# Two-layer diffusion-transformer block on eight cores: stages over all tokens, side work woven between main steps, two even FFN blocks, address tracking in place of barriers

## The chip, the cores and the metric

The kernel runs on the eight cores of one Trainium2 chip, which form two dies (cores 0 to 3 and 4 to 7). Each core computes half of the latent tokens of one of four samples, and no core waits for another. Each has a matmul engine (PE, with its weight loads shown apart as PEld), a vector engine (DVE), a scalar engine (ACT), a GpSimd engine (POOL, used here to issue the weight DMAs) and a sync engine (SP, used for the other DMAs).

The metric is the device time of the slowest core in microseconds (us). Executions come in a fast and a slow state; in the slow one the cores of one die, or of both, show a lower granted clock and the time is some per cent longer.

## The reference, cut to what matters

```python
D_MODEL, SEQ, CTX_LEN, HEAD_DIM = 2048, 4096, 256, 128
ATT_Q_HEADS, ATT_KV_HEADS, FFN_HIDDEN, WINDOW = 12, 4, 5632, 128

for i in range(2):                                   # two layers (shortened)
    mod  = silu(c) @ w_mod + b_mod                   # 6 x 2048: shift, scale, gate, twice
    cmod = silu(c_ctx) @ w_mod + b_mod               # the same for the context tokens
    xn = rms_norm(h) * (1 + scale1) + shift1
    # layer 0: q, k (per-head RMS norm, rotary), v; full attention over 256 context + 4096 latent keys;
    #          a gated width-3 convolution of 512 channels beside it
    # layer 1: the same heads, keys within 128 positions + the context keys, a learned sink per head;
    #          a multi-scale mean pooling of 512 channels beside it
    h = h + gate1 * (concat(attention, aux) @ w_out)
    hn = rms_norm(h) * (1 + scale2) + shift2
    h = h + gate2 * ((silu(hn @ w_gate) * (hn @ w_up)) @ w_down)
    # layer 0 does all this for the context tokens too; layer 1 only reads their keys and values
return rms_norm(h)                                   # latent tokens
```

A core owns 2048 latent tokens, computes 128 more and the 256 context tokens through layer 0 for the sake of layer 1's window and prefix, and needs layer-0 keys and values of all 4352 tokens.

## The kernel before: the parts that matter

A small scheduler appends instructions to one list per engine and derives semaphore waits from named buffer slots. Where buffers are reused under other names, a barrier makes every engine wait for all earlier work. **In the timelines read below, each engine executes its list in the order in which the program appended to it** (a DVE step that needs nothing of the three steps of 0.6 us before it starts only after them, and ACT stands still for 5.29 us meanwhile); everything below turns on that.

The program goes through layer 0 in three token blocks (1024, 1024 and 128 + 256), with attention, output projection and FFN in each:

```python
for b in range(3):
    c0 = 0
    for si_, sb in enumerate(subs0[2 * b:2 * b + 2]):
        stage1(0, sb, c0, mod_part=2 * b + si_)     # attention, w_out, mods, second norm
        c0 += sb["n"]
    sc.barrier()
    hcol = subs0[2 * b]["hcol"]
    segs = [(0, c0, 0)] if b < 2 else [(0, 128, 0), (128, 384, 1)]
    stage2(0, hcol, c0, segs)                       # FFN of this block
    sc.barrier()
```

The norm's second half, which writes the normalised activations, is a pair of steps per 128 channels: a multiplication on DVE, then an addition of the shift on ACT.

```python
for c in range(KD):                                 # norm_finish, 16 chunks of 128 channels
    ti = 1 + (c % 2)
    sc.op("dve", lambda e, c=c, ti=ti: e.scalar_tensor_tensor(
        out=tmp[ti][:, 0:n], in0=Xb[:, c, 0:n], scalar=dcol(acol + c), in1=tmp[0][:, 0:n],
        op0=ALU.mult, op1=ALU.mult), ...)
    sc.op("act", lambda e, c=c, ti=ti: e.activation(
        out=dst[:, c, dst_c0:dst_c0 + n], in_=tmp[ti][:, 0:n], func=AF.Identity,
        bias=dcol(bcol + c), scale=1.0), ...)
```

The key and query heads go through a three-deep pipeline, `proj_heads`. `A` is the per-head norm (square on ACT, a matmul with ones on PE, logarithm and exponential on ACT, a multiplication on DVE, a copy on ACT), `B` the rotary part (a matmul on PE, then three DVE steps).

```python
proj(0)
if ni > 1:
    proj(1)
for i in range(ni):
    A(i)
    if i + 2 < ni:
        proj(i + 2)
    B(i)
```

## Time and profile before

Four executions took 10001.53 to 10074.45 us, with a median of 10005.08 us.

| before, core 4 (the slowest of the profiled run) | |
|---|---|
| PE busy | 7548.1 us of 10077.9 (75%) |
| PE waits for w_mod tiles | 501.4 us |
| PE waits in the FFN's down product for the reloaded residual | 303.6 us |
| a dense FFN stretch, 2660 to 2968 us | 1406 matmuls in 308 us, clock 0.99 |
| the third FFN block (384 tokens), 5660 to 6400 us | PE busy 435.9 of 740 us, clock 0.78 |
| the three layer-0 FFN blocks | 1057 + 1055 + 713 = 2825 us |

The last row is read in the chain of waits, from the first wait for a gate tile to the last store of a block. The page's first lines give the busy time of the engines, then the PE row and the clock row in 40 slices of the span (digits are tenths):

```profile
span 10077.9 us, 109258 instructions; the slowest of 8 cores (9996.4 to 10077.9 us)
...
PE 7548.1 (75%) x37188; PEld 3431.9 (34%) x37188; DVE 2363.6 (23%) x4252; ACT 2513.5 (25%) x3658; POOL 529.4 (5%) x454
...
PE   2665486879897868899955456557699994679897
...
PEclk9777798989998979899976678778899997889998
```

The FFN blocks are the stretches of eights and nines in the PE row; the low slices between them are norms, mod products and attention preludes, and the run of fives in the middle holds the third FFN block. Groups of the same page, with busy time, mean ns of one, and idle time of the engine before the group with its main cause:

```profile
L450 PE MATMUL pair<-arena 128*128 128x512 bf16 (+2 forms) x624 | 282.0, 486 | 536.0 <-ACT arena L445 323.8
...
L409 PE MATMUL pair<-arena 128*128 128x2 bf16 x3072 | 87.8, 165 | 501.4 <-DMA arena<-w_mod 501.4
```

The matmuls with ones of the norms (L450) find PE idle for 536 us, nearly twice their busy time; the mod products (L409) keep PE busy 88 us and idle 501 us. Two windows, with columns as named in their first line:

```profile
core 4: us, PE busy (x) PEld busy (x) DVE busy (x) ACT busy (x) POOL busy (x), PEclk, DMA share, GB/s
2660.00:2968.00 308.00, 305.59 (x1406) 137.96 (x1407) 32.05 (x46) 23.88 (x44) 22.08 (x19) 0.99 0.57 78
5660.00:6400.00 740.00, 435.90 (x2320) 233.01 (x2320) 57.03 (x118) 27.95 (x54) 75.09 (x63) 0.78 0.94 132
```

In the dense stretch a 512-column matmul starts every 308 / 1406 = 0.219 us. In the 384-token block the DMA engines are busy 94% of the time: all FFN weights are read for few tokens.

### The profile page before, as it was taken

The page shows a single profiled execution, that of the slowest core. Times are in us where ns is not written, and L with a number is a line of the kernel's source. Part 1 is how long each engine was busy: PE and PEld are TensorE (multiplying, and loading weights), DVE is VectorE, ACT ScalarE, POOL GpSimd, SP SyncE. Part 2 cuts the span into 40 slices and gives each one's busy share as a digit, 9 for nine tenths or more (in the row PEclk, how much of TensorE's full clock was granted, in tenths as well). Part 3 has the DMA queues.
Part 4 walks back from the last instruction along what each step waited for, and adds up shares of the span by engine and source line. Part 5 has one row for each costly group of instructions (what it writes and reads, how often), then busy time and mean ns, then how long its engine had stood idle before and what let it go on. Part 6 is the DMA issues. An engine that isn't in the chain of part 4 may idle for free.

```text
span 10077.9 us, 109258 instructions; the slowest of 8 cores (9996.4 to 10077.9 us)
## 1 busy us (share of the span) xinstructions
PE 7548.1 (75%) x37188; PEld 3431.9 (34%) x37188; DVE 2363.6 (23%) x4252; ACT 2513.5 (25%) x3658; POOL 529.4 (5%) x454
## 2 busy tenths in 40 slices
PE   2665486879897868899955456557699994679897
PEld 1222232334342323344433333223244441234342
DVE  2222143421112434111122100234411113430102
ACT  2223274810002837100023100234510003430000
POOL 0000000000000000000000011000000000000000
PEclk9777798989998979899976678778899997889998
DMA  8777847375757373857677899654466666555756
GB/s 153 136 137 126 138 107 148 105 117 78 127 84 152 102 142 101 123 94 112 93 152 154 127 127 124 132 114 96 97 95 109 97 114 154 110 93 70 135 70 166
DMA packets 1251085, 1186.96 MB, mean 118 GB/s; under 512 B 54128, under 2 KB 1098352, under 8 KB 1250544
## 3 DMA queue, kind: packets, MB, share of 16 engines
q0 software_dynamic: 988320, 659.35, 48.7%
q1 hardware_dynamic: 262224, 520.62, 16.5%
q8 instruction: 312, 5.11, 0.2%
q14 instruction: 229, 1.88, 0.1%
HBM read 1684.66 MB, written 154.53 MB: 182 GB/s over the span
## 4 chain that ended last, share of the span: by engine, by line
PE 53%; DMA 33%; DVE 6%; ACT 4%; issue 3%; another core or an unknown queue 1%; SPq 0%; DVEq 0%; ACTq 0%; POOL 0%; POOLq 0%
PE pair L924 25%; DMA arena<-hT_d 8%; DMA hT_d<-arena 7%; PE pair L485 7%; PE pair L881 5%; PE pair L687 4%; PE pair L717 4%; DMA arena<-w_mod 4%; DMA arena<-w_gate 4%; DMA arena<-kT_d 2%; DVE arena L964 2%; PE pair L726 2%; DMA arena<-v_d 2%; PE pair L621 2%; ACT arena L467 2%
## 5 line engine op out<-in xcount | busy, mean ns | idle before, releaser
L924 PE MATMUL pair<-arena 128*128 128x512 bf16 (+1 forms) x12672 | 2723.8, 379 | 200.9 <-DMA arena<-w_up 139.4
L924 PEld LDWEIGHTS pair<-arena 128*128 128x128 bf16 x12672 | 1254.2, 99 | 1668.9 <-issue 279.1
L955 PE MATMUL pair<-arena 128*128 128x512 bf16 (+1 forms) x6336 | 1450.8, 394 | 321.8 <-DVE arena L964 303.6
L701 ACT ACTIVATE arena<-pair 128x1024 bf16<-128x1024 f32 (+2 forms) x1224 | 1077.5, 907 | 354.1 <-PE pair L687 250.6
L933 ACT ACTIVATE arena<-pair 128x512 f32<-128x512 f32 (+1 forms) x396 | 212.6, 583 | 3467.6 <-PE pair L924 3467.6
L485 PE MATMUL pair<-arena 128*128 128x512 bf16 (+2 forms) x4032 | 859.8, 374 | 286.2 <-ACT arena L467 246.3
L955 PEld LDWEIGHTS pair<-arena 128*128 128x128 bf16 x6336 | 641.2, 102 | 1131.4 <-issue 494.9
L687 PE MATMUL pair<-arena 128*128 128x512 bf16 (+1 forms) x2436 | 691.1, 385 | 273.9 <-DMA arena<-v_d 271.1
L936 DVE TENSOR_TENSOR arena<-pair,arena 128x512 bf16<-128x512 f32 (+1 forms) x396 | 268.0, 677 | 2551.9 <-PE pair L924 2533.3
L717 PE MATMUL pair<-arena 128*128 128x512 bf16 (+3 forms) x2436 | 678.6, 357 | 127.7 <-ACT arena L701 82.8
L445 ACT ACTIVATE arena<-arena 128x512 bf16<-128x512 f32 (+2 forms) x312 | 181.7, 582 | 2182.4 <-DMA arena<-hT_d 670.1
L450 PE MATMUL pair<-arena 128*128 128x512 bf16 (+2 forms) x624 | 282.0, 486 | 536.0 <-ACT arena L445 323.8
L485 PEld LDWEIGHTS pair<-arena 128*128 128x128 bf16 x4032 | 399.9, 103 | 705.3 <-issue 352.1
L964 DVE SCALAR_TENSOR_TENSOR arena<-pair,arena 128x512 f32<-128x512 f32 (+1 forms) x320 | 218.8, 684 | 1677.2 <-DMA arena<-hT_d 1513.0
L712 DVE TENSOR_TENSOR arena<-arena 128x512 bf16<-128x512 bf16 (+2 forms) x1080 | 416.8, 386 | 743.5 <-PE pair L717 446.2
L881 PE MATMUL pair<-arena 128*128 128x512 bf16 (+2 forms) x2560 | 524.4, 362 | 30.9 <-DMA arena<-w_out 14.3
L409 PE MATMUL pair<-arena 128*128 128x2 bf16 x3072 | 87.8, 165 | 501.4 <-DMA arena<-w_mod 501.4
L687 PEld LDWEIGHTS pair<-arena 128*128 128x128 bf16 x2436 | 243.0, 105 | 522.8 <-issue 335.4
L464 DVE SCALAR_TENSOR_TENSOR arena<-arena 128x512 f32<-128x512 f32 (+2 forms) x560 | 381.1, 686 | 144.9 <-ACT arena L457 78.9
L467 ACT ACTIVATE arena<-arena 128x512 bf16<-128x512 f32 (+2 forms) x560 | 375.2, 670 | 104.5 <-DVE arena L464 70.3
L726 PE MATMUL pair<-arena 128*128 128x512 bf16 (+2 forms) x1080 | 389.6, 361 | 11.8 <-DVE arena L712 5.8
L717 PEld LDWEIGHTS pair<-arena 128*128 128x128 bf16 x2436 | 232.3, 103 | 419.0 <-issue 244.0
(72 smaller groups left out, 3504.1 us busy)
## 6 DMA issues: line engine op xcount, KB each, us to landing
arena<-w_in POOLq DMA_DIRECT2D x61, 2048.0 KB, 21.0
arena<-w_gate POOLq DMA_DIRECT2D x110, 1024.0 KB, 10.4
arena<-w_up POOLq DMA_DIRECT2D x110, 1024.0 KB, 10.4
arena<-w_down POOLq DMA_DIRECT2D x80, 1408.0 KB, 14.7
arena<-w_mod POOLq DMA_DIRECT2D x48, 2048.0 KB, 30.9
arena<-w_out POOLq DMA_DIRECT2D x40, 2048.0 KB, 15.0
arena<-hT_d SPq DMA_DIRECT2D x132, 512.0 KB, 4.9
hT_d<-arena SPq DMA_DIRECT2D x132, 512.0 KB, 5.0
```

Of the source, the lines that this page charges most:

```text
L464: sc.op("dve", lambda e, c=c, ti=ti: e.scalar_tensor_tensor(out=tmp[ti][:, 0:n], in0=Xb[:, c, 0:n], scalar=dcol(acol + c), in1=tmp[0][:, 0:n],
L467: sc.op("act", lambda e, c=c, ti=ti: e.activation(out=dst[:, c, dst_c0:dst_c0 + n], in_=tmp[ti][:, 0:n], func=AF.Identity, bias=dcol(bcol ...
L485: ins = e.matmul(bk[:, 0:n], lhsT=wt[:, k, cc * 128:(cc + 1) * 128], rhs=src[:, k, c0:c0 + n], start=(k == 0), stop=(k == KD - 1))
L687: sc.op("pe", lambda e, bi_=bi_, k_ap=k_ap: e.matmul(banks[bi_][:, 0:n], lhsT=k_ap, rhs=qa[:, h, 0:n], start=True, stop=True), reads=[s_kv ...
L701: sc.op("act", lambda e, P3=P3, S3=S3, nb_=nb_: e.activation(out=P3[:, 0:nb_, 0:n], in_=S3[:, 0:nb_, 0:n], func=AF.Exp, scale=float(ATT_SC ...
L712: sc.op("dve", lambda e, P3=P3, pq=pq: e.tensor_tensor(out=Psum[pq][:, 0:n], in0=P3[:, 0, 0:n], in1=P3[:, 1, 0:n], op=ALU.add), reads=[s_P ...
L717: sc.op("pe", lambda e, v_ap=v_ap, ti=ti, c0=c0, c1=c1, first=first, last=last, P3=P3: e.matmul(banks[O_b][:, c0:c1], lhsT=v_ap, rhs=P3[:, ...
L726: sc.op("pe", lambda e, pq=pq, dfirst=dfirst, dlast=dlast: e.matmul(banks[D_b][:, 0:n], lhsT=ones, rhs=Psum[pq][:, 0:n], start=dfirst, sto ...
L881: ins = e.matmul(banks[bi_][:, 0:n], lhsT=wt[:, k, c * 128:(c + 1) * 128], rhs=qa[:, k, 0:n], start=(k == 0), stop=(k == KD - 1))
L924: ins = e.matmul(banks[bks[si]][:, 0:b - a], lhsT=wt[:, k, off + c2 * 128:off + (c2 + 1) * 128], rhs=hn[:, k, a:b], start=(k == 0), stop=( ...
L955: ins = e.matmul(banks[yb[si]][:, 0:b - a], lhsT=wt[:, f, c2 * 128:(c2 + 1) * 128], rhs=aT[:, f, a:b], start=(f == 0), stop=(f == 21))
L964: sc.op("dve", lambda e, si=si, a=a, x0=x0, x1=x1, j=j, yb=yb, hi_=hi_, dch=dch: e.scalar_tensor_tensor(out=hb[hi_][:, x0:x1], in0=banks[y ...
```

## The change

The intent is to keep PE fed. The kernel is rewritten so that

- each stage (keys and values, queries, gates, attention with w_out, FFN, layer-1 projections, window attention) runs over all of the core's tokens before the next one starts;
- norms, the mod products, w_out and the pooling become generators ("side" work), and a `weave` emits a given number of their steps per main step into the same instruction lists;
- layer 0's FFN takes two token blocks, 1280 and 1152, in place of three, so its weights are read twice;
- slots carry their addresses, so an access waits for whatever overlaps it and the barriers vanish;
- weights arrive from the host already cut into tiles, in rows of 4 KB and more; attention sums four exponentials before the denominator matmul in place of two, and has two score buffers in place of three.

The diff has 2340 lines. Its core, with cuts marked by "...":

```diff
-    def barrier(self, engs=("pe", "act", "dve", "sp"), skip_keys=("ring0", "ring1", "ring2", "ring3")):
...
+            for o in [s] + s.over:
+                self._wait(eng, o.w)
+                for tok in o.rs.values():
+                    self._wait(eng, tok)
...
+TB = [(0, 1280), (1280, 1152)]
+SPL0 = [[(0, 428), (428, 854), (854, 1280)], [(0, 384), (384, 768), (768, 1152)]]
...
+class Side:
...
+    def weave(self, main, rate):
+        credit = 0.0
+        for _ in main:
+            credit += rate
+            while credit >= 1.0:
+                credit -= 1.0
+                if not self.step():
+                    credit = 0.0
+                    break
...
+    def pipe(items):
...
+        for i in range(n):
+            if items[i].get("A"):
+                items[i]["A"]()
+            if i + 2 < n:
+                proj(i + 2)
+            if items[i].get("B"):
+                items[i]["B"]()
+            yield
...
+    def body():
...
+        stage_a0(side)
+        stage_b0(side)
+        side.weave(ffn_gen(0, 0), 1.6)
+        side.drain()
+        side.add(norm1_gen(0))
+        side.weave(ffn_gen(0, 1), 0.5)
+        side.drain()
+        side.add(norm1_gen(1))
+        stage_a1(side, 0)
+        side.drain()
+        stage_a1(side, 1)
+        stage_b1(side)
+        side.weave(ffn_gen(1, 0), 2.4)
```

`pipe` is the old `proj_heads` with a `yield` at the end of each round: the woven side step is emitted there, after `B(i)` and before `A(i + 1)`. A woven norm step, `apply`, is the same pair as before, DVE then ACT.

## The prediction

> **What bounds the kernel now.** TensorE (PE), and half of that by waiting. The page gives PE busy 7548 us of 10078. The groups show streams of 128x512 matmuls; windows over a dense stretch (2660 to 2968) give 1406 matmuls in 308 us, 218 ns each, at clock 0.99.[...] My estimate by counting moving columns from the code: 31,400 matmuls' worth of 512 columns, 6.8 ms[...]. The other 3.2 ms are idle time and the low clock around it. The waits show where:
> - PE L409 waits 501 us for w_mod tiles (31 us each to landing).
> - The third FFN block (384 tokens, 5660 to 6400) takes 740 us for about 343 us of matmuls; PE waits for w_gate/w_up.
> - FFN down stages take 195 to 215 us per half where 704 matmuls need 152; PE waits for DVE L964, which waits for hT reloads (304 us).
> - RMS norms before each stage: L450 waits 536 us, the first projection after a norm 246 us.
> - k/v reloads per head: L687 waits 271 us, mostly in the 128-token, context and window blocks.
> - The two final norms, about 80 to 95 us each.
>
> **What the change does.** Work falls little: denominator matmuls per quad instead of per pair (-430 units of 512 columns), fewer aux columns, one norm fewer; my count is 30,600 units, 6.6 ms, plus 48 mod tiles now streamed with N=512 (at most 3.5 us each, estimate). The gain is overlap: norms, w_out, mod and k/v loads run beside matmuls, barriers vanish, layer-0 FFN reads weights twice instead of three times with 31 to 35 us of PE work per tile, weights arrive in contiguous 4 KB rows (I expect 12 to 15 us a tile, what w_out needs today).
>
> **Stage by stage (estimates, us).**
> - Start: 8 mod tiles and a norm, 140 (now 230).
> - Layer-0 k/v with woven norm: ACT, DVE and PE all near 33 per 512 tokens; with ordering loss 50 each, 425. Queries: 60 items at the traced 4.2 plus mods, 300. Aux 215.
> - Attention: now 1.08 per key pair, PE-bound (five matmuls). It becomes 4.5, but the exponential itself takes 1.02 plus 0.05 gap, so ACT binds at 1.07: quads gain nothing directly, they make room for w_out. Each 3.5 us w_out chunk starves ACT (two score buffers instead of three). 305 per block; stage 1310, with about 30 lost to mod tiles in the first block.
> - FFN layer 0: 2189 of matmuls, 42 of w_out, 25 exposed per block for loading hn: 2305 (now about 2840).
> - Layer-1 projections 470; window attention and w_out 465.
> - FFN layer 1: 1965 (now about 2015 with final norms).
> - Last final norm: one buffer, 16 serial load-scale-store rounds of 10 to 11: 180, exposed.
> - Unforeseen stalls 105.
>
> Sum 7880 us, range 7500 to 8300; chance of faster by over 2%: 0.97, within 2%: 0.02, slower: 0.01.
>
> **What would show it.** PE busy share near 85 to 88%; FFN windows above 97% PE at clock 0.98 or more; attention windows with exponentials about 1.07 us apart between w_out chunks; w_mod waits under 100 us; no 384-token DMA-bound stage; a PE-idle tail of 150 to 200 us.
>
> **What would make it wrong.** [...]Or w_out and mod chunks placed in PE's order before their weights land, stalling attention; or woven norms delaying projection chains more than I allow; or the serial tail longer.

The 6.8 ms hold: in its densest part, from 2680 to 2880 us at clock 1.00, the trace of before has 928 matmuls of 512 columns in 200 us, 0.216 us each, so that 31,400 take 6.8 ms. Other times of matmuls are estimates of the same kind, a count by the time of one.

Other readings, with what the traces show: an exponential of 1024 columns took 1.022 us in the mean (from 1000 to 1600 us) and twelve in a row took 12.89 us (from 1399.14), 1.07 each. A tile of w_out took a median of 15.0 us to land, one of w_mod 30.9; in the changed kernel it is 19.9 and 20.4, not 12 to 15. The 33 us of the layer-0 keys and values are an estimate for which the prediction names no reading. As to the clock, all eight cores of the kernel before show 0.99 to 1.00 from 2660 to 2968 us. Each core's times count from its own start, and the record does not show when the cores start, so this does not show that they were dense at the same time.

## The result, and the profile after

Four executions of the changed kernel took 8877.16 to 9009.42 us, with a median of 8882.01 us. (In the longest, die 0 has a mean clock of 0.90 in place of 0.92.) The ratio to the kernel before is 0.8898, with a 95% interval from 0.8823 to 0.8973. (A ratio is the mean time of one kernel's fast runs over that of the other's of the same rounds, so it is not quite the ratio of the medians quoted.) It is faster, as predicted, but by about 1120 us and not by the predicted 2125: the time lies outside the predicted range of 7500 to 8300 us.

The lines of the page that answer to those shown of before:

```profile
span 8881.9 us, 100054 instructions; the slowest of 8 cores (8830.8 to 8881.9 us)
...
PE 7197.8 (81%) x35368; PEld 3419.1 (38%) x35368; DVE 2307.6 (26%) x4515; ACT 2313.1 (26%) x3352; POOL 216.9 (2%) x262
...
PE   3556897978877699998999987576556999989993
...
PEclk9778998999998899999999997797777999999996
...
L546 ACT ACTIVATE arena<-arena 128x512 bf16<-128x512 f32 (+6 forms) x448 | 281.7, 630 | 839.0 <-DVE arena L542 823.7
```

PE is busy 81% of the span, not the predicted 85 to 88%. The 384-token hole is gone and the wait for w_mod fell from 501.4 to 131.3 us. But dips remain in slices 1 to 4 and 25 to 31 (counted from one), with a low clock beside most of them: these are the start and layer 0's key stage, the layer-1 projections and the window attention. The last line, the ACT half of the woven norm, shows ACT idle for 823.7 us in front of it, waiting for its DVE half (L542).

The stages in windows (boundaries are the DMA waits that open a stage in the chain of waits): layer-0 keys and values; attention; layer-0 FFN; the two blocks of layer-1 projections; window attention; layer-1 FFN.

```profile
150.00:805.00 655.00, 382.11 (x1352) 147.54 (x1352) 230.15 (x368) 247.39 (x418) 1.75 (x2) 0.78 0.26 73
...
1337.00:2921.00 1584.00, 1250.70 (x5728) 512.34 (x5728) 690.04 (x1616) 998.39 (x1152) 34.96 (x40) 0.93 0.50 116
2921.00:5272.00 2351.00, 2245.75 (x13040) 1268.03 (x13040) 339.03 (x609) 234.20 (x399) 65.73 (x80) 0.98 0.52 111
5272.00:5792.00 520.00, 312.59 (x1184) 138.09 (x1184) 143.85 (x256) 151.03 (x282) 5.25 (x6) 0.74 0.34 84
5792.00:6027.00 235.00, 173.93 (x908) 87.46 (x908) 76.70 (x145) 82.67 (x161) 5.24 (x6) 0.91 0.55 130
6027.00:6743.00 716.00, 417.31 (x1772) 178.49 (x1772) 269.38 (x578) 241.15 (x378) 10.49 (x12) 0.77 0.40 99
6743.00:8735.00 1992.00, 1908.57 (x8783) 849.43 (x8784) 271.08 (x409) 166.12 (x245) 63.11 (x77) 0.98 0.56 121
```

The FFN stages keep PE busy for 2245.75 of 2351 us and 1908.57 of 1992 us at clock 0.98. The others hold PE for 58 to 79% of their time at clocks of 0.74 to 0.93. Against the prediction, stage by stage:

| stage | predicted, us | measured, us | missed by |
|---|---|---|---|
| start | 140 | 150 | 10 |
| layer-0 keys and values, norm woven | 425 | 655 | 230 |
| queries and mods | 300 | 328 | 28 |
| gates and convolution inputs (aux) | 215 | 204 | -11 |
| attention with w_out woven | 1310 | 1584 | 274 |
| FFN layer 0 | 2305 | 2351 | 46 |
| layer-1 projections | 470 | 755 | 285 |
| window attention with w_out woven | 465 | 716 | 251 |
| FFN layer 1 | 1965 | 1992 | 27 |
| last final norm | 180 | 147 | -33 |
| unforeseen stalls | 105 | counted in the rows above | -105 |
| sum | 7880 | 8882 | 1002 |

Four stages carry the miss, and they are the four in which ACT and DVE are busy too and a side generator with DVE and ACT steps is woven in. No one engine's busy time in the windows above fills more than 79% of such a stage. So the loss is in the waits between engines. The waits of PE, the worst first (total us, times, longest us):

```profile
PE pair L479 <- ACT arena L597: 346.0, 74, 13.5
PE pair L479 <- ACT arena L903: 260.6, 163, 5.8
PE pair L479 <- DVE arena L528: 131.6, 85, 4.0
PE pair L479 <- DMA arena<-w_mod: 131.3, 19, 11.7
```

L597 is the square of the per-head norm, L903 the attention's exponential, L528 a square of a woven norm (49.2 of its 131.6 us fall in attention, 34.7 in layer 0's key stage). The timeline shows how 0.5 us of ACT work can hold PE for four. It is one key head of the first layer-1 block (start us, duration, engine, line, operation, idle time before it and what ended that):

```profile
5327.60 5.89 PE L479 MATMUL pair<-arena 128*128 128x428 bf16 x18 [3.86 <-ACT arena L597]
...
5333.67 0.60 DVE L616 TENSOR_TENSOR arena<-pair,arena 128x428 f32<-128x428 f32 x1 [3.42 <-PE pair L479]
5334.19 0.59 DVE L618 TENSOR_TENSOR arena<-arena 128x428 f32<-128x428 f32 x1
5334.96 0.60 DVE L620 TENSOR_TENSOR arena<-arena 128x428 bf16<-128x428 f32 x1 [0.17 <-DVE arena L618]
5335.48 0.61 DVE L542 SCALAR_TENSOR_TENSOR arena<-arena 128x384 f32<-128x384 f32 x1
...
5336.19 0.61 ACT L546 ACTIVATE arena<-arena 128x384 bf16<-128x384 f32 x1 [5.29 <-DVE arena L542]
5336.71 0.51 ACT L597 ACTIVATE arena<-pair 128x426 bf16<-128x426 f32 x1
...
5337.36 6.14 PE L479 MATMUL pair<-arena 128*128 128x426 bf16 x18 [3.87 <-ACT arena L597]
```

Read it as a circle. PE runs 18 matmuls (one with ones, the 16 of the projection of item i + 2 and one rotary product) until about 5333.5. Only then can DVE do the three rotary steps of item i (L616, L618, L620). The woven norm step L542 depends on none of them but stands behind them in DVE's list. ACT's half L546 waits 5.29 us for it. The square L597 of item i + 1, whose projection has long been done, stands behind L546 in ACT's list. PE's next instruction is the matmul with ones that needs this square, so PE stands still for 3.87 us and starts the round again. A round takes 9.8 and 10.0 us here. Every matmul and every ACT and DVE step of this round starts in program order: L542 at 5335.48, after L620 at 5334.96, and L597 at 5336.71, after L546 at 5336.19.

The second thing in these lines is that the 18 matmuls take 5.9 us; the weight loads of the same timeline start 0.355 us apart, for matmuls of 426 to 428 columns. In a dense FFN stretch of the same run, at clock 1.00, matmuls of the same widths start 0.180 us apart (556 in 100 us, 3500 to 3600). So here PE runs at half of that speed. Half-microsecond windows of the same item, with PE's busy time, count and granted clock, show when:

```profile
5331.50:5332.00 0.50, 0.50 (x3) 0.50 0.00 0
5332.50:5333.00 0.50, 0.50 (x4) 0.81 0.00 0
5333.50:5334.00 0.50, 0.00 (x0) 1.00 0.00 0
5336.00:5336.50 0.50, 0.00 (x0) 0.60 0.05 19
5337.50:5338.00 0.50, 0.50 (x2) 0.50 0.00 0
```

The clock comes back to 1.00 near 5332.7, when PE has nearly finished, stays there through most of the idle gap, and is at 0.50 again before the next matmul starts. The fall comes at about 5336.1 (an estimate from the 0.60 of the window from 5336.0 to 5336.5), 3.4 us after the rise and 2.6 us after PE's last matmul. In the 3.4 us before it PE was busy for the first 0.8. The next item has the same: a rise at about 5342.9 and a fall at about 5346.3 (estimates from the windows with 0.57 and 0.84).

### The profile page after: what moved, and what is told of

Read it like the earlier page. It is cut to its first block, busy times and chain, and to the rows that moved or that the text cites. A ratio compares the mean times of both kernels' runs of the same rounds, so it can differ in the third digit from the quotient of the medians.

```text
span 8881.9 us, 100054 instructions; the slowest of 8 cores (8830.8 to 8881.9 us)
## 1 busy us (share of the span) xinstructions
PE 7197.8 (81%) x35368; PEld 3419.1 (38%) x35368; DVE 2307.6 (26%) x4515; ACT 2313.1 (26%) x3352; POOL 216.9 (2%) x262
## 4 chain that ended last, share of the span: by engine, by line
PE 72%; DMA 10%; DVE 7%; ACT 6%; issue 4%; SPq 1%; DVEq 0%; ACTq 0%; another core or an unknown queue 0%; POOL 0%; POOLq 0%
PE pair L479 72%; DMA arena<-w_mod 4%; ACT arena L903 2%; DMA arena<-hT 2%; ACT arena L546 1%; DVE arena L542 1%; DMA arena<-hn 1%; DVE arena L618 1%; DMA arena<-ud 1%; DVE arena L528 1%; DVE arena L1037 1%; DVE arena L620 1%; SPq L166 1%; DMA outT<-arena 0%; DVE arena L914 0%
## 5 line engine op out<-in xcount | busy, mean ns | idle before, releaser
L479 PE MATMUL pair<-arena 128*128 128x512 bf16 (+4 forms) x35368 | 7197.8, 369 | 1537.6 <-ACT arena L597 346.0
L479 PEld LDWEIGHTS pair<-arena 128*128 128x128 bf16 x35368 | 3419.1, 101 | 5315.8 <-issue 2366.7
L903 ACT ACTIVATE arena<-pair 128x1024 bf16<-128x1024 f32 (+2 forms) x1054 | 985.1, 968 | 480.9 <-PE pair L479 448.4
L1231 ACT ACTIVATE arena<-pair 128x512 f32<-128x512 f32 (+3 forms) x440 | 239.6, 545 | 2826.9 <-PE pair L479 2826.8
L1234 DVE TENSOR_TENSOR arena<-pair,arena 128x512 bf16<-128x512 f32 (+3 forms) x440 | 274.7, 624 | 2494.1 <-PE pair L479 2494.1
L1273 DVE SCALAR_TENSOR_TENSOR arena<-pair,arena 128x512 f32<-128x512 f32 (+3 forms) x352 | 225.7, 642 | 1066.1 <-PE pair L479 1062.2
L546 ACT ACTIVATE arena<-arena 128x512 bf16<-128x512 f32 (+6 forms) x448 | 281.7, 630 | 839.0 <-DVE arena L542 823.7
L542 DVE SCALAR_TENSOR_TENSOR arena<-arena 128x512 f32<-128x512 f32 (+6 forms) x448 | 279.3, 634 | 173.1 <-DMA arena<-hT 119.8
L606 DVE SCALAR_TENSOR_TENSOR arena<-pair,arena 128x512 f32<-128x512 f32 (+2 forms) x180 | 123.0, 683 | 423.0 <-ACT arena L604 423.0
L1037 DVE SCALAR_TENSOR_TENSOR arena<-pair,arena 128x512 f32<-128x512 f32 (+2 forms) x160 | 109.5, 684 | 449.2 <-PE pair L479 447.2
L616 DVE TENSOR_TENSOR arena<-pair,arena 128x512 f32<-128x512 f32 (+2 forms) x180 | 112.8, 626 | 381.5 <-PE pair L479 373.0
L609 ACT ACTIVATE arena<-arena 128x512 bf16<-128x512 f32 (+2 forms) x180 | 103.9, 577 | 188.7 <-DVE arena L606 188.7
L528 DVE TENSOR_TENSOR arena<-arena 128x512 bf16<-128x512 f32 (+2 forms) x144 | 95.8, 665 | 161.1 <-DMA arena<-x 93.6
L620 DVE TENSOR_TENSOR arena<-arena 128x512 bf16<-128x512 f32 (+2 forms) x180 | 112.8, 627 | 35.2 <-DVE arena L618 30.5
L525 ACT ACTIVATE arena<-arena 128x512 bf16<-128x512 f32 (+2 forms) x144 | 87.4, 607 | 122.9 <-PE pair L479 71.3
L618 DVE TENSOR_TENSOR arena<-arena 128x512 f32<-128x512 f32 (+2 forms) x180 | 111.1, 617 | 0.0
## 6 DMA issues: line engine op xcount, KB each, us to landing
arena<-w_mod POOLq DMA_DIRECT2D x48, 2048.0 KB, 20.4
arena<-w_out POOLq DMA_DIRECT2D x36, 2048.0 KB, 19.9
```

Source lines behind the costliest of these rows:

```text
L479: return e.matmul(out, lhsT=lhsT, rhs=rhs, start=start, stop=stop)
L542: sc.op("dve", lambda e, lo=lo, hi=hi, j=j: e.scalar_tensor_tensor(out=ta[:, lo:hi], in0=src[:, lo:hi], scalar=mcol(l, j, ps_, c), in1=rs[ ...
L546: sc.op("act", lambda e, lo=lo, hi=hi, j=j: e.activation(out=dst[:, lo:hi], in_=ta[:, lo:hi], func=AF.Identity, bias=mcol(l, j, pb_, c), s ...
L618: sc.op("dve", lambda e: e.tensor_tensor(out=tk[:, 0:n], in0=tk[:, 0:n], in1=cs[0], op=ALU.mult), reads=[T["s_tk"][p], s_cs[0]], writes=[T ...
L620: sc.op("dve", lambda e: e.tensor_tensor(out=ko[:, 0:n], in0=tk[:, 0:n], in1=t5[:, 0:n], op=ALU.add), reads=[T["s_tk"][p], T["s_t5"][0]], ...
L903: sc.op("act", lambda e: e.activation(out=P3(gi)[:, 0:nb, 0:n], in_=S3(gi)[:, 0:nb, 0:n], func=AF.Exp, scale=float(ATT_SCALE)), reads=[s_b ...
```

## The experiments

The theory formed from this: **the order of the woven steps in the in-order lists makes a loop through four engines, and PE's idle time in it also costs half of the clock.** The rival: these stages simply have too much ACT and DVE work, and the prediction under-counted it. A third, a risk named in the prediction, was a fall of the clock in longer dense stretches, but all eight cores hold 1.00 in a dense FFN stretch of the changed kernel's profiled run: from 3300 to 3900 us each of the eight has PE busy for 598.9 of 600 us at clock 1.00. This is rejected without a run.

The experiments ran on three further chips. The changed kernel, unedited, was run again on one of them (after_again2): its fast runs of 8896.53 and 8911.53 us are within 0.4% of the median above. Single stages scatter more: over the cores of the first run the attention stage takes 1552 to 1583 us. So differences of the total of over 1% are taken as the kernels' own, and smaller edits are judged by the time of the stage that they touch. Slow executions are left out (one slow profile is used in the last section): they lie between 8509 and 9994 us for the changed kernel and its edits, and between 10215 and 10957 us for the kernel before.

### pipe_order: the side step is emitted before the rotary part

```diff
             if i + 2 < n:
                 proj(i + 2)
+            yield
             if items[i].get("B"):
                 items[i]["B"]()
-            yield
```

The same instructions, in another order: L542 now stands before the rotary steps in DVE's list.

> Only the place of the woven step changes: it stands ahead of the rotary part B of an item, no longer behind it; every instruction is the same. Theory 'order' (the woven norm step sits in the in-order DVE and ACT queues behind B, so that the next item's square, and with it the next projection, waits once around PE, DVE and ACT; that costs both the wait and the clock): the items of the first layer-1 projection block fall from 10.2 us to 4.5 to 5.5, the block from 525 us to 290 to 340; layer-0 k/v with its woven norm from 655 to 430 to 520; total 8450 to 8600. Theory 'amount' (ACT and DVE simply have too much work in the woven stages): both stages within 30 us of what they were, total 8830 to 8930. The window attention and attention stages are the same under both.

Measured: fast runs of 8589.26 and 8601.92 us, about 290 us less than the changed kernel. The start up to the first attention block fell from 1337 to 1199 us, the first layer-1 block from 520 to 352 us; attention (1584) and the window stage (716) did not move. The same key heads in the timeline:

```profile
5206.98 0.34 PE L479 MATMUL pair<-arena 128*128 128x426 bf16 x1 [0.48 <-ACT arena L609]
5207.22 0.51 ACT L597 ACTIVATE arena<-pair 128x428 bf16<-128x428 f32 x1
5207.50 0.60 DVE L616 TENSOR_TENSOR arena<-pair,arena 128x426 f32<-128x426 f32 x1 [0.90 <-PE pair L479]
...
5207.87 3.22 PE L479 MATMUL pair<-arena 128*128 128x428 bf16 x17 [0.55 <-ACT arena L597]
...
5210.26 0.61 DVE L542 SCALAR_TENSOR_TENSOR arena<-arena 128x384 f32<-128x384 f32 x1
...
5211.25 0.34 PE L479 MATMUL pair<-arena 128*128 128x428 bf16 x1 [0.16 <-issue]
```

A round is now 4.27 us (5206.98 to 5211.25), with 17 matmuls in 3.22 us, 0.19 us each in place of 0.355. L542 still stands behind the rotary steps of the item before, but these now end early, and PE no longer waits for the chain behind it for more than about half a microsecond. In the whole block ACT's wait for L542 fell from 201.3 to 49.5 us and PE's wait for the square from 156.9 to 38.2. The block in a window, against the line of the changed kernel that starts with 5272.00:

```profile
5135.00:5487.00 352.00, 253.54 (x1184) 118.59 (x1184) 142.67 (x256) 150.64 (x282) 5.25 (x6) 0.89 0.50 124
```

The same 1184 matmuls, DVE and ACT busy within 1%, and the time fell by a third (to 352 us, a little above the 290 to 340 expected). The rival falls for the projection stages.

### apply_late: the ACT half of a norm step is emitted one step later

```diff
     def apply(...):
         ... DVE half ...
-        for (lo, hi, j) in segs:
-            sc.op("act", ... Identity ...)
+        def second():
+            for (lo, hi, j) in segs:
+                sc.op("act", ... Identity ...)
+        return second
     # callers: run the pending second(), then apply(c), keep its second() for the next step
     # sq_sum: the matmul with ones is likewise emitted one step after its square
```

This cuts the same loop at another place: when ACT and PE reach a woven step, what they need from DVE or ACT is already done.

> The woven step stays behind B, but no step holds two dependent halves any more: the ACT half of a norm's application and the ones matmul of a square are emitted one step later than the DVE half and the square. Same instructions. Theory 'order': ACT no longer stands still for a DVE result just queued, PE no longer for a square just queued. Full attention blocks from 358 us to 310 to 330, window blocks from 205 to 180 to 195, first layer-1 projection block from 525 to 300 to 380, layer-0 k/v from 655 to 480 to 580; total 8300 to 8500. Theory 'amount': every stage within 5%, total 8830 to 8930.

Measured: fast runs of 8527.42, 8530.41 and 8536.89 us; ratio to before 0.8482, interval 0.8458 to 0.8507. Attention fell from 1584 to 1429 us, the first layer-1 block from 520 to 364, the start up to attention only from 1337 to 1310 and the window stage from 716 to 697. One window of each kernel, the attention stage:

```profile
1310.00:2739.00 1429.00, 1202.30 (x5728) 499.97 (x5728) 687.05 (x1615) 990.85 (x1152) 34.96 (x40) 0.96 0.57 128
```

Against the line of the changed kernel that starts with 1337.00: the same 5728 matmuls, ACT and DVE busy within 1%, the stage 155 us shorter. This is the clearest evidence against the rival in attention: no work was removed there. The full blocks took 314 to 317 us, as expected. Not as expected: the window blocks (198 to 200 us, where 180 to 195 had been forecast) and layer 0's key stage, which became only some 30 us shorter where 75 to 175 had been forecast. The edit moves two pairs at once, the norm's halves and the square with its matmul; what each is worth was not run apart.

### norm_first: the layer-1 norm of the second block runs alone

```diff
         side.add(norm1_gen(1))
+        side.drain()
         stage_a1(side, 0)
```

> The norm of the second token block (layer 1) runs alone, ahead of the first layer-1 projections, and is not woven into them. Theory 'order': weaving cost more than it hid: the norm alone takes 150 to 220 us, the projections then need 240 to 290 (items of 3.6 to 4.2 us), in sum 400 to 500 against 525 woven; total 8780 to 8870. Theory 'amount' (an engine is full in the woven stage): taking the overlap away must make it longer, 600 or more, total 8950 or more.

Measured: one fast run of 8850.16 us. The norm alone takes 164 us with PE idle, and the projections after it 297 us at clock 0.94, together 461 us; woven they took 520. So in the changed kernel weaving cost more there than doing the two in sequence. With the order repaired (pipe_order) weaving costs 352 us, only 55 above the projections alone.

### fill and fill_heads: useless matmuls that keep the clock up

```diff
+        def filler():
+            def f(e):
+                for k in range(20):
+                    ins = mm(e, banks[7][:, 0:384], ones, sx[:, k % 16, 0:384], True, True)
+                return ins
+            sc.op("pe", f, reads=[s_cb] + s_xn1, writes=[s_bank[7]])
-        side.weave(pipe(items), 1.0)
+        side.weave(pipe(items, filler if tb == 0 else None), 1.0)
```

Twenty matmuls into an unused bank follow every item (fill), or every item with a rotary part (fill_heads), of the first layer-1 block. The loop stays; what is meant to change is the clock.

> Work is added, nothing taken away: 20 matmuls of 384 columns into an unused bank after each item of the first layer-1 projection block, where PE stood idle. Theory 'clock' (about 40% of an item's 10.2 us is the half clock that follows PE's idle stretches: 18 matmuls at 0.355 us in place of 0.18): with PE kept busy the clock there rises from 0.73 to 0.95 or more and the items get SHORTER, 7 to 8.5 us, the block 400 to 460 us, total 8800 to 8850. If the clock is only a sign and not a cause, items stay at 10 us or grow to 13, total 8880 to 9100.

> The filler again, now only after the items that idle (heads); in the first filler run the token items, which leave PE no idle time, grew by 20 x 3.3 us and hid the gain. Theory 'clock': the first layer-1 block falls below the 520 us of the kernel without any filler, to 450 to 490, although PE does 960 matmuls more; granted clock there 0.93 or more against 0.74. If the clock is no cause: 520 or more.

Measured, fill: one fast run of 8974.21 us; the block took 542 us, not less than 520, so the expectation for the block failed. Its clock rose to 0.96 and the key and query heads fell from 10.0 to 7.95 us each, but the value and pooling items, which had no half-clock loop, grew by 3.25 us each. That asked for the second run. (The total of fill is no clean measure: it is that of core 7, which in this run has a mean clock of 0.921 where cores 0 to 3 have 0.926 to 0.929.)

Measured, fill_heads: a fast run of 8876.11 us (another was slow), with this block:

```profile
5285.00:5761.00 476.00, 400.13 (x2144) 206.01 (x2144) 144.85 (x256) 150.39 (x281) 5.25 (x6) 0.96 0.37 92
```

It holds 2144 matmuls where the changed kernel has 1184, and takes 476 us where that takes 520. This is what the clock theory had expected (450 to 490 us, clock 0.93 or more). More work in less time leaves the clock as the cause of that part: nothing else was seen that added work could help. Of the 5.7 us by which an item of the changed kernel (10.0) exceeds one of pipe_order (4.3), about 2 are the clock (10.0 to 7.95) and the rest the loop; this split is an estimate from the two items, since the filler itself may delay a round.

### both_rate: both orders, and fewer side steps per round in layer 0's key stage

```diff
-        side.weave(pipe(items), 6.0)
+        side.weave(pipe(items), 4.2)
```

The edits of pipe_order and apply_late, and this line.

> Both orders together (woven step ahead of B; dependent halves one step apart), and the layer-0 norm woven at 4.2 steps an item in place of 6, so that it spreads over all items of a block instead of the first five. If order is the whole cause in the projection stages, layer 0 up to the start of attention falls from 1337 us to 1080 to 1150 (1199 with the first order alone), the first layer-1 block from 520 to 320 to 350, attention stays at the 1430 and the window stage at the 697 of the second order alone; total 8230 to 8380. If the two orders remove the same wait twice, layer 0 stays at 1190 or more.

Measured: a fast run of 8394.82 us. The start up to attention took 1165 us, the first layer-1 block 357, attention 1437. Start, block and total miss their expected ranges by 7 to 15 us, on the slow side. The first edit is worth 290 us alone, the second 350, both with the rate 490: they cut the same loop in the first layer-1 block (352, 364, 357 us there), so their gains don't add there. Up to attention they nearly do (138 and 27 us alone, 172 together with the rate); what the rate is worth by itself was not run.

### fin_late: the finish of a window head one group later

The window stage was the one that no order so far had moved. In its finish, DVE adds the sink, ACT takes a logarithm and an exponential, DVE multiplies, all emitted together after the denominator matmul; ACT's logarithm waits for DVE in front of the next exponential.

```diff
                 sc.op("dve", ... add sink ...)
-                sc.op("act", ... Ln ...)     # and Exp, and the DVE multiplication
+                fin_q.append(lambda: fin2(ui, True))
...
             softmax(gi)
+            while fin_q:
+                fin_q.pop(0)()
```

> Only in the attention finish with a sink (window stage): the logarithm on ACT is emitted one key group later than the DVE addition whose result it reads. Theory 'order' (ACT stands still 53 us per window block for that addition, exponentials behind it wait, PE waits for them): window blocks from 204 us to 165 to 185, window stage from 716 to 600 to 660, total 8770 to 8830. If PE's own chain (projection chunk, then DVE, one bank) sets the pace: blocks at 195 or more.

Measured: a fast run of 8855.36 us (two others were slow). The window stage fell from 716 to 664 us, its blocks from 204 to 206 us each to 190 to 192. The direction was right, the size was missed: 165 to 185 us per block had been expected, and 195 or more by the rival that PE's own chain sets the pace. In the window stage ACT's wait for the addition fell from 192.0 to 50.2 us and PE's wait for the exponential from 86.8 to 44.0. A wait of PE that stayed explains part of what is left:

```profile
PE pair L479 <- DVE arena L955: 58.2, 30, 3.9
```

L955 is the addition of the sink. All heads share one PSUM bank for their denominators, so PE waits for DVE to have read it before the next head may start; that wait did not change (57.1 us in the changed kernel). The edit cut ACT's wait, not this one.

### apart2: w_out drained before the attention of its block

```diff
+            side.drain()
             for lp in (mods[0:2] if b == 0 else mods[b + 1:b + 2]):
                 side.add(mod_gen(*lp))
             side.weave(attn_gen(units), 0.34 if b < 4 else 0.8)
```

The same in front of the window stage's weave, where the pooling is drained too. (The late mods of full attention stayed woven, because the drain comes before they are added; the recorded text says otherwise and is wrong in that.) This asks what the changed kernel's weaving of w_out is worth at all.

> The output projection (and the pooling and late mods beside it) is drained before the attention of the same block starts, in both attention stages, so nothing is woven. Theory (the order of steps in the queues costs the time): in sequence a full-attention block takes about 335 us (about 225 attention, 110 output projection), no longer than the 358 us woven, a window block about 195 us against 204, and a fast run of the whole about 8790 to 8880 us. Rival (the stage has that much work for its engines, and weaving does hide part of it): a full-attention block takes 420 us or more and the whole 9100 us or more.

Measured: a fast run of 8941.28 us, 1590 us for the attention stage against 1584 woven, 776 for the window stage against 716. One full-attention block in windows, first the drained w_out, then attention:

```profile
2000.00:2115.00 115.00, 72.17 (x288) 27.31 (x286) 31.92 (x46) 22.00 (x31) 3.50 (x4) 0.85 0.71 150
2115.00:2353.00 238.00, 213.44 (x1009) 83.75 (x1008) 129.27 (x315) 209.89 (x227) 3.49 (x4) 0.98 0.38 90
```

A block in sequence takes 353 us (2000 to 2353), woven 358 to 362. In full attention weaving as the changed kernel did it gained next to nothing, as the theory said (over the cores the stage takes 1577 to 1594 us in sequence and 1552 to 1583 woven, so 10 us or so can't be read from it), though the sequence took 353 and not 335 us; the mods that stayed woven may account for some of the difference. In the window stage weaving was worth 60 us (blocks of 219 to 225 us in sequence, 204 to 206 woven), where the theory had expected the sequence to be faster; it was wrong there. The rival's 420 us per block and 9100 us in all did not come. With the order repaired the same weave saves about 160 us over the sequence in full attention (1429 in apply_late against 1590; a sequence with the repaired order was not run, so part of these 160 may be the repair of the drained steps themselves). So weaving paid in full attention only once the woven steps were ordered so that no engine's next step waits for a chain through the others.

### best1: all of it

The orders, the rate of 4.2 and fin_late; the pooling input of a window block is loaded one block ahead (PE had waited 74.0 us for it in four waits); the mod steps in the first attention block are spread (rate 0.09 in place of 0.34); and the last final norm uses four buffers in place of one.

```diff
-            side.weave(attn_gen(units), 0.34 if b < 4 else 0.8)
+            side.weave(attn_gen(units), 0.09 if b == 0 else 0.34 if b < 4 else 0.8)
...
+                if g == 3 and b + 1 < 4:
+                    ub_load(b + 1)
...
-        for _ in final_gen(1):
-            pass
+        final_tail(1)
```

> All of these orders, and three more repairs of waits seen in the trace: the pooling input is fetched one block ahead (PE waits 13 to 20 us per block for it), the eight modulation tiles of the first attention block are spread over the whole block (PE waits for them, 35 to 40 us to landing each), the last final norm has four buffers in place of one (147 us tail). Layer 0 to attention 1080 to 1150, attention 1350 to 1400, window stage 540 to 610, tail 70 to 90; total 7950 to 8180.

Measured: a fast run of 8118.11 us. Start up to attention 1161, attention 1399, first layer-1 block 352, window stage 579, last norm 56 us in place of 147.

### best_timed2, best_timed3 and after_again2

The same kernel timed, and the changed kernel beside it.

> The same kernel as best1, timed. If the reordered steps are worth what the single look said, fast runs lie between 8080 and 8160 us and the ratio to the kernel before is about 0.81. The rival, that the single look was a lucky run, expects fast runs at 8300 us or more, ratio 0.83 or more.

> The changed kernel itself, unedited, on the chip of these runs, so that the edits are compared on one chip: fast runs 8850 to 8910 us and a ratio to the kernel before of about 0.885 if the chips agree; if this chip is quicker by itself, 8700 us or less.

> The kernel best1 once more, in five rounds: on the chip of best_timed2 only one of its six executions was fast (8116.55 us) and none of the kernel before, so that no ratio came out. If this chip gives both kernels fast executions, the fast runs lie between 8080 and 8160 us and the ratio is about 0.81; if the reordering only shifts work into the slow state, fast executions stay above 8300 us.

Measured, best_timed2: five of six executions were slow (8509.31 to 9152.77 us), the sixth took 8116.55 us, so there is no ratio. Measured, after_again2: fast runs of 8896.53 and 8911.53 us. On core 5 its stages are within 1% of the first run's, except attention with 1559 us against 1584, which is the scatter over cores named above. Measured, best_timed3: five fast runs of 8119.28 to 8130.65 us (and one slow), two fast ones of the kernel before (10072.42 and 10122.22): ratio 0.8045, interval 0.8009 to 0.8080. This version beats both kernels. Its page (core 1, the slowest) and its waits of PE (core 5):

```profile
PE 7031.5 (87%) x35368; PEld 3371.1 (41%) x35368; DVE 2296.7 (28%) x4515; ACT 2292.2 (28%) x3352; POOL 216.9 (3%) x262
...
PE   3778888988986999998999997686668999989996
```

```profile
PE pair L481 <- ACT arena L920: 138.0, 153, 3.2
PE pair L481 <- DMA arena<-w_mod: 121.7, 14, 12.4
...
PE pair L481 <- ACT arena L610: 77.5, 63, 9.5
PE pair L481 <- DVE arena L972: 60.3, 30, 3.5
```

PE is busy 87% of the span. The wait for the square (L610 here, L597 before) fell from 346.0 to 77.5 us, that for the exponential (L920, before L903) from 260.6 to 138.0; that for the sink (L972) stays at 60.3.

## Why the prediction was wrong, and where it was right

**Right: the direction, and what bounds the kernel.** PE idle time and the low clock around it were the cost, and the named causes went: waits for w_mod fell from 501.4 to 131.3 us (though under 100 had been predicted), and no DMA-bound 384-token stage is left.

**Right: the FFN.** 2305 and 1965 us were predicted, 2351 and 1992 measured, at clock 0.98. The windows show PE busy for 95.5% and 95.8%, a little under the predicted 97%. The stage alone went from 2825 to 2351 us in layer 0, over 40% of the whole gain.

**Right: queries, aux and the last norm**, each within 35 us. These have little woven work or none.

**Right in outcome: the clock in dense stretches did not decide the result.** Its fall was named as a risk; the profiled run of the changed kernel holds 1.00 from 3300 to 3900 us on all eight cores. Why it should fall or not was not shown; a slow run does show 0.81 (see the last section).

**Wrong: "ACT, DVE and PE all near 33 per 512 tokens; with ordering loss 50 each, 425".** The sums of ACT and DVE were near enough (29 and 27 us per 512 tokens, an estimate from the stage's busy times; PE's 45 include the low clock, 0.78 over the stage), but the allowance for ordering was a guess of half again. The stage took 655 us, with PE busy for only 382.11 of them, ACT for 247.39 and DVE for 230.15. The order was the loss: pipe_order, which only moves one `yield`, took 138 us out of the time up to attention, and with the other orders and the lower rate it fell by 172 us, to 1165 (predicted for these stages together: 1080).

**Wrong: "305 per block; stage 1310".** The argument was that ACT binds at 1.07 us per group and that a chunk of w_out costs ACT a pause. Without side work the trace does show 43 exponentials in 50 us (1950 to 2000), 1.16 us each. With it there are 29 (1800 to 1850), 1.72 us each: not only the chunks but the woven norm steps stop ACT, which waits for DVE, and PE starves behind it. Blocks took 358 to 362 us. apply_late, at equal work, took 155 of the missing 274 us out. The base was mis-sized too: with 1.16 in place of 1.07 us, the stage's 896 exponentials need some 80 us more (an estimate). This could have been read blind: the trace of before has 85 exponentials in 100 us (1400 to 1500), 1.18 each, where the prediction wrote 1.08 from counting matmuls.

**Wrong: "Layer-1 projections 470; window attention and w_out 465".** These were 755 and 716. Of the 285 us in the first, pipe_order alone took out 163. For the second, fin_late took out 52, and with prefetch and the other orders best1 reached 579. Here part of the loss is not weaving at all but the main chain's own order in the finish of a head; with w_out drained the stage took longer (776).

The step that failed is the same in all of these: a stage with two woven chains was costed by the busy time of its engines (in attention, of ACT alone) plus an allowance or a pause, and not by the waits between them. What has to be asked is the length of one round through the lists: which instruction of each engine stands in front of the one that the next engine needs. Here one round was 10.0 us, and 4.3 us for the same work in another order. The prediction's last paragraph named the right risk ("woven norms delaying projection chains more than I allow") without costing it; counting the round (three rotary steps of 0.6 us, a norm pair of 0.6 each, a square of 0.5) gives 3.5 of the 3.9 us of idle PE per item. The trace of before has the same kinds of step (its norm pair took 686 and 670 ns in the mean of all shapes, in groups L464 and L467), so this could have been done blind.

**What the balance is, and what stays open.** PE's busy time fell by 350 us with 1820 fewer matmuls, and its idle time by about 850 (2530 to 1684 us); 1002 us more were expected in all. best1 recovers 764 us of the 1002, of which 91 are the last norm, which was not mis-predicted. Some 100 us each in the window stage and the layer-1 projections and 80 to 90 in each of the other two stages, against the prediction, remain in best1. For the window stage the shared denominator bank is part of it (PE waits 60.3 us for L972 in best_timed3). For attention the mis-sized exponential would account for most of it, for the layer-1 projections PE's waits for the loads of their input for part (45.5 us for xn in the changed kernel, 44.7 in best_timed3). No run here tested these, and for layer 0's key stage the remainder is open.

**What is argued and not shown.** The clock rose to 1.00 at about 5332.7 and again at about 5342.9, 10.2 us apart, where a round of the loop takes 9.8 to 10.0 us, and each time it fell again 3.4 us later. That the loop kept in step with the rises and falls, and so stayed slow, fits this but was not tested apart.

## What to carry to other kernels

Before weaving side work into a main loop, write down each engine's list for one round and follow the circle: wherever a woven step on engine X waits for engine Y, everything behind it on X waits too (here the square of 0.5 us behind ACT's wait of 5.29 us). Emit the dependent half of a woven pair one step later, and put woven steps ahead of those of the main loop that wait for the end of PE's work; in this kernel both left the work as it was. When a stage has a low clock beside modest idle time, look for a loop of a few microseconds per item, because curing the loop gave back much of the clock here as well (0.74 to 0.89 in the first layer-1 block).

## What the traces show of the clock

- In the changed kernel's profiled run all eight cores held 1.00 for 600 us of dense matmuls (PE busy 598.9). In the slow profile of best_timed2 it was otherwise. Core 6 shows it in two windows of dense FFN work, one before and one after about 6150 us; cores 0 to 3 kept a mean of about 0.956 in the same run, cores 4 to 7 one of 0.905 to 0.908. The matmuls of the second window are wider, so only the clock column is to be compared:

```profile
2800.00:3000.00 200.00, 200.00 (x1111) 1.00 0.39 78
6800.00:7000.00 200.00, 198.67 (x749) 0.81 0.36 63
```

  From 6200 to 8400 us core 6 shows 0.81 in every window of 200 us but one (0.77 from 7200 to 7400). What brings this clock about, and why on one die, the record doesn't show. (This was seen, not tested.)
- In the kernel before, 1406 pairs of weight load and matmul took 308 us, 0.219 us each, and 928 of them in the densest 200 us, 0.216 each.
- In the loop of the changed kernel a burst of 6 us in every 10 ran at the half clock almost throughout, with the full clock granted in the idle gap (0.50 from 5327 to 5332.5, 1.00 from 5333 to 5336), and the clock fell at about 5336.1, with PE busy for about 0.8 of the 3.4 us before. That added matmuls shorten a stage is measured here (476 us with 2144 matmuls, 520 with 1184).
